# Windowed attention of a two-layer block: two heads' scores on the two halves of the array's rows, and transposed weights as the stationary operand against values laid high and low part side by side

## Chip, cores and metric

The kernel runs on one core of a Trainium2 chip, as one launch. The metric is the device time of that launch in microseconds (us). All arrays are float32. Products that must be exact to float32 are made from fp32r operands: a number is split into a high part (what a cast to fp32r keeps) and a low part (the rest), and three products, high·high, high·low and low·high, are summed in PSUM.

## The reference, cut to what matters

A block of depth 2 on 512 tokens and 256 context tokens, width 1024. Layer 0 has a gated MLP beside differential attention, layer 1 has the attention below; both are followed by a SwiGLU feed-forward stage (hidden 2816). Only layer 1's attention is touched:

```python
C_HEADS, C_KV_HEADS, HEAD_DIM, WINDOW, Q_BLOCK = 16, 4, 64, 128, 128   # 4 query heads to a key/value head
def sink_attend(q, kvs, sink):
    scores = []
    for k, v, mask in kvs:                      # the window's keys, then the 256 context keys
        s = einsum('bqhgd,bkhd->bhgqk', q, k) * ATTN_SCALE
        if mask is not None:
            s = where(mask, s, NEG_INF)
        scores.append(s)
    p = softmax(concatenate(scores + [s_sink], axis=-1), axis=-1)
    out = None                                  # sum over kvs of p's part @ v
    ...
def block(args):                                # one of 4 blocks of 128 queries
    kb, vb = 384 keys and values around the block      # 256 for the first and the last block
    mask = in range & (abs(qpos - kpos) <= WINDOW)
    return sink_attend(qb, [(kb, vb, mask), (kc, vc, None)], sink)
y = o.reshape(b, s_len, 1024) @ w_out
```

## The kernel before

Everything is kept transposed (features on partitions, tokens along the row). `odd()` is layer 1's mixer. It projects keys (`project_k`), values (six tiles of 128 tokens, one for each token block), and queries (`project_q(n)`, n = 0..7, two heads each: 24 products of 128x512 into the single PSUM bank of `fill()`). `attend(g, half)` then does one group of four heads (they share keys and values) for two of the four query blocks i. It calls `softmax(g, i, rc)` for the scores and the exponentials of the four heads x, and then goes over the key blocks kb, 4 of them for an edge block (i = 0 or 3) and 5 for an inner one (i = 1 or 2): 16 calls of `softmax`, 72 key blocks in all.

- Scores. `stack_q` puts one head's 64 high rows and 64 low rows on top of each other, `stack_k` writes the high keys on both halves and the low keys on both halves. A head's scores are then two products that use all 128 rows of the array, for the window's keys (L1150) and for the context's keys (L1158); window blocks other than the diagonal one get a mask added by a product of a mask with the identity (L1155). An edge block has 256 window keys, so one two-bank PSUM tile (`wide()`, two of them) holds two heads; an inner one has 384, and each head takes a `wide()` of its own. VectorE takes the row maximum (L1161), ScalarE the exponentials and their sums (L1164).
- Values. For each key block the four heads' exponentials are transposed into one PSUM bank (L1186, four products of 128x128), split into high part (ScalarE, L115) and low part (VectorE, L116), and multiplied by `mm3` (L99, L100, L101): the stationary operand is 64 columns of the values, the moving operand the 512 columns of four heads, and the output has 64 partitions.
- Normalization. The reciprocal sums are spread over 64 columns by GpSimd (L1197) and transposed (L1201); ScalarE copies the outputs out of PSUM (L1194) and VectorE multiplies (L1203). `keep` splits the result for the output projection `project(half, ...)`, products of 128x256 (L99 to L101 again, moving operand `ax`, weights through `blocks` and `unit`, whose splits are L75 and L78).

The order of instructions on each engine is set before the run by a list scheduler that works on the program with its own time estimates. It uses the output projection of half 0 and the query projections as filler between the attention's products. Tiles are handed out from pools; PSUM has 8 banks: three single ones (`bank()`, tiles `pb`), one `fill()` (`pf`), and two double ones (`wide()`, `pw`).

Of the kernel before, what the change touches and what calls it, by code (L numbers as in the profile page):

```python
# [6 lines left out]
F32 = mybir.dt.float32  # L7
# [7 lines left out]
P = 128  # L15
# [11 lines left out]
class Builder:  # L27
# [1042 lines left out]
    def odd(self):  # L1070
# [33 lines left out]
        vhi, vlo = [], []  # L1104
# [19 lines left out]
        def project_q(n):  # L1124
            ps = self.fill()
            self.dense(ps, self.blocks(a["q1"][n]), X)
            qf = Rs.tile([P, TX], F32, name=self.uid("qf"), tag="qf", bufs=2)
            self.rope(ps, qf, tabs)
            Qs[n] = self.stack_q(qf, Rs, TX, "sq", 16, 0.125)

        def softmax(g, i, rc):
# [9 lines left out]
            for x in range(4):  # L1141
                pair, par = x // 2, x % 2
                if edge:
                    two = self.wide() if par == 0 else two
                    ps = two[:, par * TX:par * TX + TX]
                else:
                    ps = self.wide()
                Q = Qs[2 * g + pair][par][:, i * P:(i + 1) * P]
                for p in range(2):
                    nc.tensor.matmul(ps[:, st:en], Q, K[g][p][:, b0 * P:b1 * P], start=p == 0, stop=p == 1,  # L1150
                                     skip_group_check=True)
                for b in range(b0, b1):
                    if b != i:
                        m0, c = (b - i + 1) * P, st + (b - b0) * P
                        nc.tensor.matmul(ps[:, c:c + P], identr, mask[:, m0:m0 + P], start=False, stop=True,  # L1155
                                         skip_group_check=True)
                for p in range(2):
                    nc.tensor.matmul(ps[:, en:en + TC], Q, K[g][p][:, TX:], start=p == 0 and not edge, stop=p == 1,  # L1158
                                     skip_group_check=True)
                c = nm[:, x:x + 1]  # L1160
                nc.vector.tensor_reduce(c, ps[:, st:en + TC], axis=AX, op=ALU.max, negate=True)  # L1161
                nc.vector.tensor_tensor(c, c, nsink[:, 4 * g + x:4 * g + x + 1], ALU.min)
                e = Rs.tile([P, 640], F32, name=self.uid("e"), tag="e1", bufs=7)
                nc.scalar.activation(e[:, :w + TC], ps[:, st:en + TC], AF.Exp, bias=c, accum_out=sums[:, x:x + 1])  # L1164
                es.append(e)
# [6 lines left out]
        def part(dtype=F32R):  # L1172
            return Rs.tile([P, 512], dtype, name=self.uid("pt"), tag="pt", bufs=6)

        def attend(g, half):
            raw[half, g] = Rs.tile([P, 2, TC], F32, name=self.uid("o"), tag="o", bufs=4)
            rc = self.small(8, "rc", 3)
            for i in (2 * half, 2 * half + 1):
                es, b0, b1 = softmax(g, i, rc[:, i % 2 * 4:i % 2 * 4 + 4])
                po = self.bank()[0:64, :]  # L1180
                nb = b1 - b0 + 2
                for kb in range(nb):
                    vb = b0 + kb if kb < b1 - b0 else 4 + kb - (b1 - b0)
                    pt = self.bank()
                    for x in range(4):
                        nc.tensor.transpose(pt[:, x * P:(x + 1) * P], es[2 * (x % 2) + x // 2][:, kb * P:(kb + 1) * P],  # L1186
                                            self.ident)
# [149 lines left out]
```

## Time and profile before

| what | value |
|---|---|
| median of the runs | 1698.41 us (1693.54 to 1702.56, 3 runs) |
| the profiled execution | 1697.54 us |
| its span, first to last instruction | 1695.8 us |
| TensorE busy, weight loads busy | 1558.7 us (92%), 1379.5 us (81%) |
| VectorE, ScalarE, GpSimd busy | 1145.4, 752.8, 806.8 us |
| mean granted TensorE clock | 0.972 |
| layer 1's attention in the span | about 1030 to 1250 us |

In the rows, PE is TensorE's products, PEld its weight loads (they overlap products), DVE VectorE, ACT ScalarE, POOL GpSimd. A product is shown as out<-moving operand, stationary operand (in alphabetical order), the rows and columns of the array that it uses (128*64), and the moving shape. The duration of one product contains its latency, so neighbours overlap; what a product costs TensorE is read from start to start in the timeline.

### The profile page before, as it was taken

Reading aid. Unit: us, or ns where it says so; the run is one execution under the profiler, and the core shown is the slowest. Engines: PE = TensorE matmul, PEld = TensorE weight load, DVE = VectorE, ACT = ScalarE, POOL = GpSimd, SP = SyncE. Lnnn points to the kernel's source line nnn. Section 1 sums busy time; section 2 is a strip of 40 time slices with the busy share of each in tenths; the row PEclk is TensorE's granted clock in tenths of the full one; section 3 lists DMA queues with packets and bytes.
Section 4 is the critical chain, followed back from the end, with each engine's and each line's share of the span. In section 5 each row is a group of like instructions: output and inputs, shape, how many; then the busy total and the mean of one; then the engine's idle time right before and its main releaser. Section 6 shows DMA issues by size and latency. Waiting matters only on the chain.

```text
span 1695.8 us, 24602 instructions
## 1 busy us (share of the span) xinstructions
PE 1558.7 (92%) x9415; PEld 1379.5 (81%) x9415; DVE 1145.4 (68%) x2037; ACT 752.8 (44%) x1521; POOL 806.8 (48%) x586
## 2 busy tenths in 40 slices
PE   6999989798899999999999988999987898999996
PEld 4776878698798889888899977778866788888986
DVE  4613788856967677666765676777769865756566
ACT  3413676433533233333333345676655444444443
POOL 0562211232675566656665336512115665666673
PEclk9999989899899899999999999999998999999998
DMA  8753100241032343344341112101140322222311
GB/s 312 290 184 133 32 1 1 87 159 41 25 125 88 124 136 110 127 136 135 132 132 38 49 63 75 51 7 45 50 146 10 125 90 98 87 100 78 110 38 50
DMA packets 47958, 161.98 MB, mean 96 GB/s; under 512 B 5472, under 2 KB 9952, under 8 KB 40160
## 3 DMA queue, kind: packets, MB, share of 16 engines
q1 hardware_dynamic: 47696, 160.28, 27.6%
q8 instruction: 74, 1.21, 0.3%
q14 instruction: 44, 0.36, 0.1%
q10 hardware_dynamic: 144, 0.13, 0.0%
HBM read 158.29 MB, written 2.10 MB: 95 GB/s over the span
## 4 chain that ended last, share of the span: by engine, by line
PE 65%; DVE 18%; DMA 6%; ACT 4%; issue 3%; POOL 3%; POOLq 0%; SPq 0%; DVEq 0%; ACTq 0%
PE pb L100 9%; PE pb L101 9%; PE pb L99 9%; PE pw L99 8%; PE pw L100 8%; PE pw L101 7%; DMA raw<-ffn_in 6%; POOL w L904 3%; DVE t L925 2%; PE pf L99 2%; PE pf L100 2%; PE pf L101 2%; PE pf L349 2%; DVE sq L925 1%; PE pb L1186 1%
## 5 line engine op out<-in xcount | busy, mean ns | idle before, releaser
L78 POOL TENSOR_TENSOR w<-raw,w 128x512 fp32r<-128x512 f32 (+1 forms) x84 | 128.6, 1540 | 234.3 <-ACT w L75 211.8
L99 PE MATMUL pw<-ax,w 128*128 128x384 f32 (+2 forms) x648 | 211.9, 331 | 18.0 <-DVE q L972 5.7
L904 POOL TENSOR_TENSOR w<-t,w 128x512 fp32r<-128x512 f32 x106 | 156.4, 1476 | 149.1 <-ACT w L901 146.0
L100 PE MATMUL pw<-ax,w 128*128 128x384 f32 (+2 forms) x648 | 210.7, 326 | 2.7 <-DVE ax L456 1.4
L101 PE MATMUL pw<-ax,w 128*128 128x384 f32 (+2 forms) x648 | 208.4, 324 | 3.1 <-DVE w L904 3.1
L757 DVE SCALAR_TENSOR_TENSOR xT<-pb,mod,xT 128x512 f32<-128x512 f32 (+3 forms) x208 | 143.9, 703 | 68.3 <-PE pb L101 67.9
L904 POOL TENSOR_TENSOR w<-raw,w 128x512 fp32r<-128x512 f32 x111 | 155.7, 1414 | 59.2 <-ACT w L901 59.2
L99 PE MATMUL pb<-hh,w 128*128 128x512 f32 x480 | 167.4, 363 | 14.8 <-ACT hh L115 7.9
L100 PE MATMUL pb<-hh,w 128*128 128x512 f32 x480 | 172.3, 361 | 0.7 <-POOL hh L116 0.2
L99 PE MATMUL pw<-T,w 128*128 128x384 f32 (+1 forms) x504 | 158.7, 318 | 12.2 <-DVE hs L968 9.5
L101 PE MATMUL pb<-hh,w 128*128 128x512 f32 x480 | 168.7, 359 | 0.0
L901 ACT CAST w<-t 128x512 fp32r<-128x512 f32 x120 | 74.2, 620 | 208.1 <-DVE t L925 176.8
L100 PE MATMUL pw<-T,w 128*128 128x384 f32 (+1 forms) x504 | 159.1, 316 | 7.0 <-DVE T L116 4.1
L101 PE MATMUL pw<-T,w 128*128 128x384 f32 (+1 forms) x504 | 158.3, 314 | 0.0
L99 PEld LDWEIGHTS pw<-ax,w 128*128 128x128 f32 x648 | 125.0, 194 | 32.8 <-DVE q L972 9.2
L100 PEld LDWEIGHTS pw<-ax,w 128*128 128x128 f32 x648 | 125.3, 193 | 10.5 <-DVE ax L193 3.3
L101 PEld LDWEIGHTS pw<-ax,w 128*128 128x128 f32 x648 | 124.8, 193 | 6.4 <-DVE w L904 3.3
L904 POOL TENSOR_TENSOR w<-rawo,w 128x512 fp32r<-128x512 f32 x74 | 107.2, 1448 | 39.1 <-ACT w L901 39.1
L99 PEld LDWEIGHTS pb<-hh,w 128*128 128x128 f32 x480 | 90.6, 191 | 28.5 <-ACT hh L115 9.0
L99 PEld LDWEIGHTS pw<-T,w 128*128 128x128 f32 x504 | 97.3, 194 | 18.9 <-DVE hs L968 11.9
L99 PE MATMUL pb<-ax,w 128*128 128x256 f32 (+1 forms) x344 | 106.8, 313 | 4.1 <-ACT w L75 2.2
L100 PE MATMUL pb<-ax,w 128*128 128x256 f32 (+1 forms) x344 | 106.3, 309 | 2.1 <-DVE ax L116 2.1
(381 smaller groups left out, 4324.4 us busy)
## 6 DMA issues: line engine op xcount, KB each, us to landing
raw<-ffn_in SPq DMA_DIRECT2D x44, 1024.0 KB, 5.7
ar<-ada SPq DMA_DIRECT2D x24, 1024.0 KB, 7.0
ar<-ada SPq DMA_DIRECT2D x48, 512.0 KB, 3.5
rawo<-ffn_out SPq DMA_DIRECT2D x44, 512.0 KB, 3.8
raw<-odd_out SPq DMA_DIRECT2D x32, 256.0 KB, 2.7
raw<-qk SPq DMA_DIRECT2D x16, 256.0 KB, 7.8
raw<-uv SPq DMA_DIRECT2D x16, 256.0 KB, 2.7
raw<-even_out SPq DMA_DIRECT2D x8, 512.0 KB, 3.5
```

What stands on the lines that cost most here:

```text
L78: eng.tensor_tensor(lo, raw, hi.bitcast(F32), ALU.subtract)
L99: mm(out, s[0], m[0], start=start, stop=False, **kw)
L100: mm(out, s[0], m[1], start=False, stop=False, **kw)
L101: mm(out, s[1], m[0], start=False, stop=stop, **kw)
L349: nc.tensor.matmul(ps[32 * q:32 * q + 32, :w], cst[:, k, :], t[:, w * q:w * q + w], start=k == 0, stop=k == KT - 1, skip_group_check=True)
L757: self.nc.vector.scalar_tensor_tensor(h, ps[:, r], self.modcol(l, j, m, who), h, ALU.mult, ALU.add)
L901: nc.scalar.copy(t[:, 0, :], src)
L904: eng.tensor_tensor(t[:, 1, :], src, t[:, 0, :].bitcast(F32), ALU.subtract)
L925: nc.vector.tensor_tensor(t, x, y, how)
L1186: nc.tensor.transpose(pt[:, x * P:(x + 1) * P], es[2 * (x % 2) + x // 2][:, kb * P:(kb + 1) * P], self.ident)
```

## The change

Three parts of `odd()` are rewritten. The reference's result is computed as before; only the product low·low, which the stacked scores included, is left out.

1. Queries are no longer stacked. High and low parts are two plain 128-row tiles, with one head of the pair on rows 0 to 63 and the other on rows 64 to 127 (one ScalarE and one VectorE instruction on 128 rows in place of two and two on 64). The scores of a pair of heads are made from three products of 64 rows each (high·high, high·low, low·high), for window and context keys: 12 products for the pair, which alternate between the two heads and so between the two halves of the array's rows; they were 8 of 128 rows. `issue_after` fixes their order among themselves. An inner block's pair needs both `wide()` tiles from its first two products on.
2. High and low values stand side by side (`v`, 64 + 64 columns for a group). For each head and key block, the transposed exponentials are now the stationary operand: the high part against 128 moving columns (both value parts), the low part against 64. A key block takes 8 products in place of 3.
3. The output now has queries on partitions. ScalarE copies the part that came from the low values, VectorE adds it to the other, GpSimd multiplies by the reciprocal sums, the result is transposed (as many transposes as the sums needed before) and ScalarE copies it out of PSUM.

```diff
         for tb in range(6):
-            hv, lv = [Rk.tile([P, TC], F32R, name=f"v1_{p}_{tb}") for p in range(2)]
-            self.split(hv, lv, acc[tb])
-            vhi.append(hv)
-            vlo.append(lv)
+            v = Rk.tile([P, 4, 2, 64], F32R, name=f"v1_{tb}")
+            self.split(v[:, :, 0, :], v[:, :, 1, :], acc[tb].rearrange("p (g d) -> p g d", d=64))
+            V.append(v)
...
-            Qs[n] = self.stack_q(qf, Rs, TX, "sq", 16, 0.125)
+            hi, lo = [Rs.tile([P, TX], F32R, name=self.uid("qs"), tag="sq", bufs=16) for _ in range(2)]
+            nc.scalar.mul(hi, qf, 0.125)
+            nc.vector.scalar_tensor_tensor(lo, qf, 0.125, hi.bitcast(F32), ALU.mult, ALU.subtract)
+            Qs[n] = hi, lo
...
-            for x in range(4):
-                pair, par = x // 2, x % 2
+            for pair in range(2):
                 if edge:
-                    two = self.wide() if par == 0 else two
-                    ps = two[:, par * TX:par * TX + TX]
+                    two = self.wide()
+                    pss = [two[:, h * TX:h * TX + TX] for h in range(2)]
                 else:
-                    ps = self.wide()
-                Q = Qs[2 * g + pair][par][:, i * P:(i + 1) * P]
-                for p in range(2):
-                    nc.tensor.matmul(ps[:, st:en], Q, K[g][p][:, b0 * P:b1 * P], start=p == 0, stop=p == 1,
-                                     skip_group_check=True)
...
-                for p in range(2):
-                    nc.tensor.matmul(ps[:, en:en + TC], Q, K[g][p][:, TX:], start=p == 0 and not edge, stop=p == 1,
-                                     skip_group_check=True)
...
+                    pss = [self.wide() for _ in range(2)]
+                last = None
+                for p, (qp, kp) in enumerate(((0, 0), (0, 1), (1, 0))):
+                    Q, Kp = Qs[2 * g + pair][qp], K[g][kp]
+                    for dst, src in ((slice(st, en), slice(b0 * P, b1 * P)), (slice(en, en + TC), slice(TX, TA))):
+                        for h, ps in enumerate(pss):
+                            r = slice(64 * h, 64 * h + 64)
+                            with tc.issue_after(last.ins) if last else ExitStack():
+                                last = nc.tensor.matmul(ps[:, dst], Q[r, i * P:(i + 1) * P], Kp[r, src],
+                                                        start=p == 0 and not (edge and dst.start == en), stop=p == 2,
+                                                        skip_group_check=True)
+                for h, ps in enumerate(pss):
+                    x = 2 * pair + h
...
-            rc = self.small(8, "rc", 3)
+            both = self.tmp("t")
             for i in (2 * half, 2 * half + 1):
-                es, b0, b1 = softmax(g, i, rc[:, i % 2 * 4:i % 2 * 4 + 4])
-                po = self.bank()[0:64, :]
+                rc = self.small(4, "rc", 3)
+                es, b0, b1 = softmax(g, i, rc)
+                po = self.bank().rearrange("p (x c d) -> p x c d", x=4, c=2)
...
                     self.split(th, tl, pt)
-                    V = [v[vb][:, 64 * g:64 * g + 64] for v in (vhi, vlo)]
-                    self.mm3(po, V, (th, tl), kb == 0, kb == nb - 1)
-                pov = po.rearrange("p (h a q) -> p h a q", h=2, q=P)
-                for par in range(2):
-                    nc.scalar.copy(raw[half, g][64 * par:64 * par + 64, :, i % 2 * P:i % 2 * P + P], pov[:, par, :, :])
+                    for x in range(4):
+                        c = slice(x * P, (x + 1) * P)
+                        nc.tensor.matmul(po[:, x, :, :], th[:, c], V[vb][:, g, :, :], start=kb == 0 and x == 0,
+                                         stop=False, skip_group_check=True)
+                        nc.tensor.matmul(po[:, x, 0, :], tl[:, c], V[vb][:, g, 0, :], start=False,
+                                         stop=kb == nb - 1, skip_group_check=True)
+                t = self.tmp()[:, :TC].rearrange("p (x d) -> p x d", d=64)
+                o = both[:, i % 2 * TC:i % 2 * TC + TC].rearrange("p (x d) -> p x d", d=64)
+                nc.scalar.copy(t, po[:, :, 1, :])
+                nc.vector.tensor_tensor(o, po[:, :, 0, :], t, ALU.add)
+                nc.gpsimd.tensor_tensor(o, o, rc.unsqueeze(2).to_broadcast([P, 4, 64]), ALU.mult)
             ps = self.bank()
-            rows = part(F32)
-            nc.gpsimd.tensor_copy(rows.rearrange("p (x d) -> p x d", d=64), rc.unsqueeze(2).to_broadcast([P, 8, 64]))
...
-            o = raw[half, g].rearrange("p a q -> p (a q)")
-            nc.vector.tensor_tensor(o, o, ps, ALU.mult)
+            raw[half, g] = Rs.tile([P, 2, TC], F32, name=self.uid("o"), tag="o", bufs=4)
+            nc.scalar.copy(raw[half, g].rearrange("p a q -> p (a q)"), ps)
```

In the changed kernel the score products are L1157, the masks L1165, the transposes L1194, the value products L1199 (high part) and L1201 (low part), the last transposes L1211.

The scheduler places the new products. On TensorE before, a key block in group 0 (`pt` are the split transposed exponentials, `v` the values, `e` the exponentials, `ident` the identity):

```order
L99 MATMUL pb_9406<-pt_9424,v_0_1_9241 64x512
L1186 MATMUL pb_9431<-ident_97,e_9372 128x128
L1186 MATMUL pb_9431<-ident_97,e_9391 128x128
L1186 MATMUL pb_9431<-ident_97,e_9381 128x128
L1186 MATMUL pb_9431<-ident_97,e_9400 128x128
L100 MATMUL pb_9406<-pt_9425,v_0_1_9241 64x512
L101 MATMUL pb_9406<-pt_9424,v_1_1_9242 64x512
```

On TensorE now, a key block of the same group, with the transposes of the next one behind it:

```order
L1199 MATMUL pb_9404<-v_4_9249,pt_9444 128x128
L1201 MATMUL pb_9404<-v_4_9249,pt_9445 128x64
L1199 MATMUL pb_9404<-v_4_9249,pt_9444 128x128
L1201 MATMUL pb_9404<-v_4_9249,pt_9445 128x64
L1199 MATMUL pb_9404<-v_4_9249,pt_9444 128x128
L1201 MATMUL pb_9404<-v_4_9249,pt_9445 128x64
L1199 MATMUL pb_9404<-v_4_9249,pt_9444 128x128
L1201 MATMUL pb_9404<-v_4_9249,pt_9445 128x64
L1194 MATMUL pb_9456<-ident_97,e_9370 128x128
L1194 MATMUL pb_9456<-ident_97,e_9375 128x128
L1194 MATMUL pb_9456<-ident_97,e_9393 128x128
L1194 MATMUL pb_9456<-ident_97,e_9398 128x128
```

Three products of 512 columns became eight of 128 and 64; the four transposes stay. The shapes shown are those of the output: 64 partitions before, 128 now.

On TensorE before, the scores of one head of an inner block (`kh` and `kl` are the stacked keys, `qb` the stacked queries):

```order
L1150 MATMUL pw_9493<-kh_8980,qb_9354 128x384
L1150 MATMUL pw_9493<-kl_8981,qb_9354 128x384
L1155 MATMUL pw_9493<-mask,identr 128x128 x2
L1158 MATMUL pw_9493<-kh_8980,qb_9354 128x256
L1158 MATMUL pw_9493<-kl_8981,qb_9354 128x256
```

On TensorE now, the scores of both heads of that pair, all but the first product (`qs_9345` is the high part, `qs_9346` the low part):

```order
L1157 MATMUL pw_9508<-kh_8980,qs_9345 128x384
L1157 MATMUL pw_9507<-kh_8980,qs_9345 128x256
L1157 MATMUL pw_9508<-kh_8980,qs_9345 128x256
L1157 MATMUL pw_9507<-kl_8981,qs_9345 128x384
L1157 MATMUL pw_9508<-kl_8981,qs_9345 128x384
L1157 MATMUL pw_9507<-kl_8981,qs_9345 128x256
L1157 MATMUL pw_9508<-kl_8981,qs_9345 128x256
L1157 MATMUL pw_9507<-kh_8980,qs_9346 128x384
L1157 MATMUL pw_9508<-kh_8980,qs_9346 128x384
L1157 MATMUL pw_9507<-kh_8980,qs_9346 128x256
L1157 MATMUL pw_9508<-kh_8980,qs_9346 128x256
L1165 MATMUL pw_9507<-mask,identr 128x128 x2
```

The two heads alternate (`pw_9507` is the one, on rows 0 to 63, `pw_9508` the other). The first product of the pair stands further ahead on TensorE, alone between products that use all 128 rows, where it waits for the first of the two `wide()` tiles only:

```order
L1199 MATMUL pb_9404<-v_1_9240,pt_9427 128x128
L1157 MATMUL pw_9507<-kh_8980,qs_9345 128x384
L99 MATMUL pf_10054<-ax_8611,w_10057 128x512
L100 MATMUL pf_10054<-ax_8612,w_10057 128x512
L101 MATMUL pf_10054<-ax_8611,w_10057 128x512
```

The 32 groups of 12 products stand in 55 uninterrupted stretches of the changed order; 32 of these come right behind transposes.

More of the change, by code (lines that the diff above doesn't have):

```diff
@@ L1185, in attend @@
                     for x in range(4):
[L1186 to L1187 removed]
+                        nc.tensor.transpose(pt[:, x * P:(x + 1) * P], es[x][:, kb * P:(kb + 1) * P], self.ident)
                     th, tl = [part() for _ in range(2)]
                     self.split(th, tl, pt)
[L1190 removed]
@@ L1198, in attend @@
             for i in range(2):
                 for pair in range(2):
-                    x = (i * 2 + pair) * P
-                    nc.tensor.transpose(ps[:, pair * TC + i * P:pair * TC + (i + 1) * P], rows[:, x:x + P], self.ident)
-            o = raw[half, g].rearrange("p a q -> p (a q)")
-            nc.vector.tensor_tensor(o, o, ps, ALU.mult)
+                    nc.tensor.transpose(ps[:, pair * TC + i * P:pair * TC + (i + 1) * P], both[:, i * TC + pair * P:i * TC + (pair + 1) * P],
+                                        self.ident)
```

29 lines of the change are left out of this document (14 added, 15 removed).

## The prediction

> **What bounds the kernel now.** First the page's busy times and the shares of the chain that ended last, to see which engine sets the end; then the stretches around layer 1's attention and TensorE's waits there.
>
> ```profile
> PE 1558.7 (92%) x9415; PEld 1379.5 (81%) x9415; DVE 1145.4 (68%) x2037; ACT 752.8 (44%) x1521; POOL 806.8 (48%) x586
> PE 65%; DVE 18%; DMA 6%; ACT 4%; issue 3%; POOL 3%; POOLq 0%; SPq 0%; DVEq 0%; ACTq 0%
> ```
>
> ```profile
> 1030.00:1070.00 40.00, 34.61 (x162) 28.65 (x163) 24.81 (x43) 17.71 (x36) 26.59 (x20) 0.96 0.22 66
> 1070.00:1210.00 140.00, 135.49 (x893) 112.88 (x892) 104.27 (x219) 95.62 (x224) 41.39 (x39) 1.00 0.13 39
> ```
>
> ```profile
> PE pf L99 <- DVE qf L244: 6.3, 5, 2.5
> PE pw L1150 <- ACT e L1164: 3.7, 9, 1.4
> ```
>
> The columns of the stretches are start and end, length, the busy time of PE, PEld, DVE, ACT and POOL (instructions in brackets), the granted clock and the DMA share. In the middle of the attention PE is busy 135.5 of 140 us at full clock, DVE 104, ACT 96. So TensorE is the bound there: time added to its products lengthens the kernel nearly one for one, and DVE and ACT have a quarter of the stretch to spare. The waits (total, times, longest, us, over 1030 to 1250) show what could be won otherwise: 10 us together, the larger part in the query projections, where the next projection needs the one `pf` bank that the rope still reads (L244).
>
> What a product costs TensorE is read from start to start:
>
> ```profile
> 1132.20 0.60 PE L1186 MATMUL pb<-ident,e 128*128 128x128 f32 x4
> 1132.55 0.36 PE L1150 MATMUL pw<-kh,qb 128*128 128x256 f32 x1
> 1132.76 0.28 PE L1150 MATMUL pw<-kl,qb 128*128 128x256 f32 x1
> 1132.87 0.22 PE L1155 MATMUL pw<-mask,identr 128*128 128x128 f32 x1
> 1132.93 0.33 PE L1158 MATMUL pw<-kh,qb 128*128 128x256 f32 x1
> 1133.10 0.28 PE L1158 MATMUL pw<-kl,qb 128*128 128x256 f32 x1
> 1133.22 0.40 PE L99 MATMUL pb<-pt,v 128*64 128x512 f32 x1
> 1133.45 0.39 PE L100 MATMUL pb<-pt,v 128*64 128x512 f32 x1
> 1133.68 0.39 PE L101 MATMUL pb<-pt,v 128*64 128x512 f32 x1
> 1133.91 0.27 PE L1186 MATMUL pb<-ident,e 128*128 128x128 f32 x1
> ...
> 1147.15 0.34 PE L1150 MATMUL pw<-kh,qa 128*128 128x384 f32 x1
> 1147.32 0.34 PE L1150 MATMUL pw<-kl,qa 128*128 128x384 f32 x1
> 1147.51 0.33 PE L1155 MATMUL pw<-mask,identr 128*128 128x128 f32 x2
> ```
>
> A 512-column product takes 0.23 us (1133.22 to 1133.91 is three), a 384-column one 0.18 (1147.15 to 1147.51 is two). The four from 1132.76 to 1133.22 take 0.115 each although one has 128 columns and three have 256: below 256 columns the moving operand no longer sets the price. A transpose takes 0.0875 (1132.20 to 1132.55 is four), and the product behind a run of transposes 0.21 in place of 0.115.
>
> **The values (part 2).** What sets 0.115 is seen in the weight loads (mean ns at the end of the first number group):
>
> ```profile
> L101 PEld LDWEIGHTS pf<-ax,w 128*128 128x128 f32 x120 | 23.1, 192 | 2.6
> L1186 PEld LDWEIGHTS pb<-ident,e 128*128 128x128 f32 x288 | 35.3, 140 | 10.7 <-DVE o L1203 0.4 <-ACT o L1194 0.4
> L101 PEld LDWEIGHTS pb<-pt,v 128*64 128x64 f32 x72 | 9.7, 135 | 1.9
> ```
>
> Loading 128 columns of an fp32r operand takes 192 ns, 64 columns of the values 135. Before, one short load fed 512 columns. Now the split exponentials are loaded, 128 columns each time, for 128 or 64 moving columns: every one of the eight products should cost the load-bound 0.115. A key block goes from 3 × 0.23 = 0.69 us to 8 × 0.115 = 0.92, and with 72 key blocks (the x72) that is 72 × 0.23 = **+16.6 us**. From below, the price is bounded by the transposes' 0.0875: 8 × 0.0875 = 0.70, +0.7 us in all. I take 0.115, since the mask is the nearest row: fp32r operands, 128 moving columns. No row has 64 moving columns; they need not cost more than the 128 of the mask.
>
> **The scores (part 1).** By the same prices, a pair of heads had 8 products: 8 × 0.115 = 0.92 us in an edge block, 4 × 0.18 + 4 × 0.115 = 1.18 in an inner one; there are 16 pairs of each. Now there are 12. If the two row halves work at the same time, they take the time of 6: 0.69 and 0.885, which saves 16 × 0.23 + 16 × 0.295 = **-8.4 us**. If they queue, 12 cost 1.38 and 1.77: +16.8 us. The masks stay as they are. No row of this trace has 64-row products, but layer 0's modulation puts four products side by side on column strips (128*32):
>
> ```profile
> 61.89 0.13 PEld L349 LDWEIGHTS pf<-ar,cst 128*32 128x32 f32 x4 [0.30 <-issue]
> 62.32 0.13 PEld L349 LDWEIGHTS pf<-ar,cst 128*32 128x32 f32 x4 [0.30 <-issue]
> ...
> 16.27 0.64 PE L349 MATMUL pf<-ar,cst 128*32 128x256 f32 x8
> 16.84 0.71 PE L374 MATMUL pw<-ar,ones 128*128 128x128 f32 x4
> 17.48 0.64 PE L349 MATMUL pf<-ar,cst 128*32 128x256 f32 x8
> ...
> 19.81 1.02 PE L175 MATMUL pb<-q,ones 128*128 128x512 f32 x2
> 20.76 0.64 PE L349 MATMUL pf<-ar,cst 128*32 128x256 f32 x8
> ```
>
> Groups of four with 512 columns follow each other every 0.43 us (61.89, 62.32), while one product of that kind on the whole array takes 0.475 (two from 19.81 to 20.76). So four strips cost the time of one, and their four loads fit into 0.13 us. I take the overlap for row halves too. [...]
>
> **Changing the array's division.** In the same rows a round of 8 strip products and 4 whole ones takes 1.21 us (16.27 to 17.48). The strips are two groups of 256 columns, half of 0.43 each, so 0.43; the four others 4 × 0.115 = 0.46; what is left, 0.32, is two changes, 0.16 each. The other bound is nothing: going to the values' 128*64 products and back costs no extra time (0.12 at 1133.10, 0.23 at 1133.68). The new scores stand in 55 stretches; each has an end, and 23 of them a beginning that is not behind transposes, where 0.1 is paid already. That is 78 changes, 0 to 12.5 us. With one near row on each side I take half, **+6.2 us**. [...]
>
> **Two PSUM tiles at once.** An inner pair now holds both `wide()` tiles.
>
> ```profile
> L1161 DVE TENSOR_REDUCE sa<-pw 128x1 f32<-128x640 f32 x32 | 26.0, 816 | 5.4 <-PE pw L1158 5.2
> L1164 ACT ACTIVATE e<-pw,sa 128x640 f32<-128x640 f32 x32 | 25.5, 796 | 8.0 <-DVE sa L1162 6.8 <-DVE sa L1168 0.5 <-PE pb L1186 0.3
> ```
>
> From the pair's last product to both tiles free: two maxima (1.63), the small step on the second and the exponentials (0.8), about 2.8 us. TensorE's own work beside one pair is half a block, 2.5 key blocks of 0.35 (transposes) + 0.92 = 3.2 us. That covers it on average by little, and the products queued behind a waiting L1157 (values, transposes, projections) wait along. Between nothing and 0.5 us for each of 16 pairs, 8 us, I take **+3**.
>
> **Queries and tail.** Splitting one projection's queries cost DVE two instructions on 64 rows; now it is one on 128, nearest row L193:
>
> ```profile
> L259 DVE SCALAR_TENSOR_TENSOR qa<-qf,qa 64x512 fp32r<-64x512 f32 x8 | 8.1, 1018 | 16.0 <-ACT qa L253 15.9
> L259 DVE SCALAR_TENSOR_TENSOR qb<-qf,qb 64x512 fp32r<-64x512 f32 x8 | 5.5, 687 | 0.2
> L193 DVE SCALAR_TENSOR_TENSOR ax<-t,mod,ax 128x512 fp32r<-128x512 f32 x8 | 5.9, 744 | 0.0
> ```
>
> That is 1018 + 687 - 744 = 0.96 us less ahead of the next rope, at five waits of L99 on L244: at most -4.8 us; half, **-2.4**, as not every wait stands behind it. At the end of the attention the last group goes through copy, add, multiplication, transposes and copy before `keep`:
>
> ```profile
> L1194 ACT COPY o<-pb 64x256 f32<-64x256 f32 x32 | 11.7, 365 | 9.1 <-PE pb L101 8.6
> L1203 DVE TENSOR_TENSOR o<-o,pb 128x512 f32<-128x512 f32 x8 | 5.4, 681 | 1.0 <-ACT o L1194 1.0
> L116 POOL TENSOR_TENSOR ax<-o,ax 128x256 fp32r<-128x256 f32 x11 | 8.0, 738 | 33.1 <-ACT ax L115 33.1
> ```
>
> Before: two copies and one multiplication, 1.4 us. Now, with 256-column steps of about 0.4 (ACT), 0.4 (DVE) and 0.74 (POOL), 0.2 for two transposes and 0.7 for a 512-column copy, 2.4: **+1** once, and nothing if the output projection's products, which need no result of the last group, hide it. In the earlier groups other groups' products hide it.
>
> **Sum.** 16.6 - 8.4 + 6.2 + 3 - 2.4 + 1 = +16.0 us on the profiled execution's 1697.5 (span 1695.8 plus 1.7 around it), 1713.5. The median is 0.9 us above that execution: **1714.4 us**.
>
> **Rivals.** A: the halves queue. For it: a 64-row load still has 128 columns, and this trace has no such row. The scores then cost +16.8 in place of -8.4: 1739.6. It decides as soon as a pair of an edge block takes over 0.92 us. B: the halves overlap, and neither the changes nor the PSUM tiles cost anything (as with 128*64 products): 16.6 - 8.4 - 2.4 + 1 = +6.8, 1705.2, no change. For it: the 10 us of waits, some of which longer products can fill. C, faster: weight loads of the split exponentials run at the transposes' pace, also 128 columns. The values cost +0.7, the scores -8.4, the queries up to -4.8, changes, tiles and tail nothing: -12.5, 1685.9. It decides where a key block's eight products stay under 0.69 us. Against it stands the 192 ns of every fp32r load. D: the new order itself waits more (values and maxima fall apart): beyond 1742.
>
> **How the numbers follow.** Forecast 0.50, A 0.19, B 0.17, C 0.11, D 0.03. A measurement of this kernel can tell about 0.5%, 8.5 us. The unknown prices alone carry the forecast from about +7 to +27 (changes 0 or 12.5, tiles 0 or 8). The range takes in B and A and leaves out C and D: 1700 to 1742. Slower by over 0.5% are the forecast, A and D; within 0.5% B; faster C.
>
> **What would show it.** Right: L1199 and L1201 starting every 0.115 us, a pair's L1157 starting in twos, a longer gap where L1157 begins or ends, PE busy for longer in the attention, and everything behind it shifted. Wrong: eight value products in 0.7 us (C), L1157 every 0.115 or more (A), or PE idle in front of L1157 for over 8 us (tiles).

## The result

| | before | after |
|---|---|---|
| median | 1698.37 us (1693.54 to 1702.56, 4 runs) | 1783.65 us (1773.07 to 1797.39, 4 runs) |
| profiled execution | 1697.54 us | 1797.39 us |
| span | 1695.8 us | 1794.9 us |
| mean granted TensorE clock | 0.972 | 0.926 |

The ratio is 1.0508 (1.0426 to 1.059): slower, 85 us against the 16 that were forecast, and outside the range. The profiled execution of after is the slowest of its four runs; the others have clocks of 0.931 to 0.936. Two kernels below (`e5_low128`, `e9_spread_low128`) spread by over 1.5% from run to run: their ratios leave out the runs furthest from their fastest, and their traces are of runs that are left out.

The page of after, busy times, granted clock in 40 slices (45 us each), and the chain:

```profile
PE 1655.3 (92%) x9903; PEld 1479.6 (82%) x9903; DVE 1134.6 (63%) x2037; ACT 746.0 (42%) x1505; POOL 810.9 (45%) x594
PEclk9999989899899999999999998657858899999998
PE 65%; DVE 16%; DMA 6%; POOL 5%; ACT 4%; issue 3%; POOLq 0%; SPq 0%; DVEq 0%; ACTq 0%
```

The same row of the page of before:

```profile
PEclk9999989899899899999999999999998999999998
```

Share of busy time and chain hardly differ from before: PE 92%, 65% of the chain. By these two lines nothing happened but more PE time. The clock row tells it: the six slices from 1077 to 1346 us stand at 8, 6, 5, 7, 8, 5 where before had 9, and they are the attention. The stretches of after (start and end, length, PE busy with products in brackets, granted clock, DMA share, GB/s):

```profile
1070.00:1100.00 30.00, 29.05 (x183) 1.00 0.18 54
1100.00:1140.00 40.00, 36.70 (x215) 0.68 0.04 14
1140.00:1180.00 40.00, 39.71 (x197) 0.54 0.03 7
1180.00:1220.00 40.00, 40.00 (x198) 0.50 0.00 0
1220.00:1260.00 40.00, 39.73 (x295) 0.87 0.15 47
```

From 1180 to 1220 PE is busy for 40.00 of 40 us, and the granted clock is 0.50: half speed, without a gap. The waits of PE between 1030 and 1350 (total, times, longest) are no larger than those of before (13 us in all, against 14 before from 1030 to 1250; three rows of them here):

```profile
PE pf L99 <- DVE qf L244: 5.6, 4, 2.5
PE pb L1201 <- DVE pt L116: 4.9, 8, 1.2
PE pw L1157 <- ACT e L1171: 0.9, 3, 0.4
```

The attention as a whole, from the first score product to the last transposes, before:

```profile
1039.30:1247.90 208.60, 196.24 (x1232) 1.00 0.15 49
```

and after:

```profile
1045.60:1350.40 304.80, 293.65 (x1739) 0.73 0.10 34
```

It grew by 96.2 us; the span by 99.1. (The first score product stands 6.3 us later, and what follows the attention is 3.4 us shorter.) Length times clock estimates the time that the same work would take at full clock; it scales the waits along, 13 us of the 304.80, so it is rough: 304.80 × 0.73 = 222.5 against 208.60, **+14 us**. The other 304.80 × 0.27 = **82 us is the clock**. These figures are of the profiled execution, 100 us slower than that of before; the medians are 85 us apart.

The single prices stand in the timeline of PE (start, duration, line). Where the clock is 1.00:

```profile
1078.74 0.30 PE L1199 MATMUL pb<-v,pt 128*128 128x128 f32 x1
1078.88 0.24 PE L1201 MATMUL pb<-v,pt 128*128 128x64 f32 x1
1078.96 0.30 PE L1199 MATMUL pb<-v,pt 128*128 128x128 f32 x1
...
1080.30 0.66 PE L1194 MATMUL pb<-ident,e 128*128 128x128 f32 x4
1080.88 0.44 PE L1157 MATMUL pw<-kh,qs 64*128 64x384 f32 x2
1081.11 0.33 PE L1157 MATMUL pw<-kl,qs 64*128 64x384 f32 x1
1081.16 0.28 PE L1157 MATMUL pw<-kh,qs 64*128 64x256 f32 x1
...
1081.95 0.66 PE L1165 MATMUL pw<-mask,identr 128*128 128x128 f32 x4
...
1136.92 0.45 PE L1199 MATMUL pb<-v,pt 128*128 128x128 f32 x1
1137.17 0.36 PE L1201 MATMUL pb<-v,pt 128*128 128x64 f32 x1
1137.35 0.45 PE L1199 MATMUL pb<-v,pt 128*128 128x128 f32 x1
```

A high and a low value product together take 0.22 us at 1078.74; the same pair takes 0.43 at 1136.92. Nothing waits in either place.

What changed in the surroundings is read from the groups by shape (count, busy time and mean ns) in one stretch, 1140 to 1180. Before:

```profile
L99 PE MATMUL pf<-ax,w 128*128 128x256 f32 x26 | 7.7, 295 | 0.0
L99 PE MATMUL pb<-pt,v 128*64 128x512 f32 x17 | 7.1, 418 | 0.0
```

After:

```profile
L1199 PE MATMUL pb<-v,pt 128*128 128x128 f32 x42 | 17.2, 430 | 0.0
L1201 PE MATMUL pb<-v,pt 128*128 128x64 f32 x43 | 15.0, 351 | 0.3 <-DVE pt L116 0.3
L99 PE MATMUL pf<-ax,w 128*128 128x256 f32 x2 | 1.0, 522 | 0.0
```

Before, 512-column value products and three lines of 256-column projections (26 on L99 alone) ran between the transposes. After, there are two on L99, and the rest is transposes, scores and products of 128 and 64 columns, each behind a load of 128 columns that takes 0.31 us (mean of the 84 loads of L1199 and L1201 there, at a mean clock of 0.54). So two things changed in that stretch: each product streams fewer columns for the time that it takes, and the projections that used to stand between them were used up earlier. Theories for the clock follow from that; the experiments tell them apart.

### The profile page after: what moved, and what is told of

Its sections match the earlier page's. It is cut to its first block, busy times and chain, and to the rows that moved or that the text cites. A ratio compares the mean times of both kernels' runs of the same rounds, so it can differ in the third digit from the quotient of the medians.

```text
span 1794.9 us, 25592 instructions
## 1 busy us (share of the span) xinstructions
PE 1655.3 (92%) x9903; PEld 1479.6 (82%) x9903; DVE 1134.6 (63%) x2037; ACT 746.0 (42%) x1505; POOL 810.9 (45%) x594
## 3 DMA queue, kind: packets, MB, share of 16 engines
q8 instruction: 77, 1.26, 0.3%
## 4 chain that ended last, share of the span: by engine, by line
PE 65%; DVE 16%; DMA 6%; POOL 5%; ACT 4%; issue 3%; POOLq 0%; SPq 0%; DVEq 0%; ACTq 0%
PE pb L100 7%; PE pb L99 7%; PE pb L101 7%; PE pw L99 7%; PE pw L100 7%; PE pw L101 7%; DMA raw<-ffn_in 6%; POOL w L904 3%; PE pb L1199 3%; PE pw L1157 3%; DVE t L925 2%; PE pf L99 2%; PE pb L1194 2%; PE pf L100 2%; PE pf L101 2%
## 5 line engine op out<-in xcount | busy, mean ns | idle before, releaser
L99 PE MATMUL pw<-ax,w 128*128 128x384 f32 (+2 forms) x648 | 212.4, 331 | 20.2 <-DVE q L972 8.1
L99 PE MATMUL pb<-hh,w 128*128 128x512 f32 x480 | 166.4, 361 | 13.6 <-ACT hh L115 8.0
L99 PE MATMUL pw<-T,w 128*128 128x384 f32 (+1 forms) x504 | 158.1, 317 | 9.9 <-DVE hs L968 6.5
L99 PEld LDWEIGHTS pw<-ax,w 128*128 128x128 f32 x648 | 125.1, 194 | 34.8 <-DVE q L972 11.6
L904 POOL TENSOR_TENSOR w<-rawo,w 128x512 fp32r<-128x512 f32 x74 | 105.8, 1429 | 38.5 <-ACT w L901 38.5
L99 PEld LDWEIGHTS pb<-hh,w 128*128 128x128 f32 x480 | 89.9, 190 | 27.1 <-ACT hh L115 9.1
L99 PE MATMUL pb<-ax,w 128*128 128x256 f32 (+1 forms) x344 | 109.0, 319 | 3.0 <-ACT w L75 1.6
L99 PEld LDWEIGHTS pw<-T,w 128*128 128x128 f32 x504 | 96.8, 193 | 16.5 <-DVE hs L968 8.5
L100 PE MATMUL pb<-ax,w 128*128 128x256 f32 (+1 forms) x344 | 107.9, 314 | 2.1 <-DVE ax L116 2.1
```

The costliest lines, as they stand in the source:

```text
L99: mm(out, s[0], m[0], start=start, stop=False, **kw)
L100: mm(out, s[0], m[1], start=False, stop=False, **kw)
L904: eng.tensor_tensor(t[:, 1, :], src, t[:, 0, :].bitcast(F32), ALU.subtract)
```

## The experiments

The theory, the author's: in this kernel the granted clock goes with how many moving columns go through the array per microsecond, and not with whether TensorE is busy (40.00 us of 40 at 0.50 above). The columns of one key block (four transposes of 128 columns, then the value products) by the time that it takes at full clock are the measure. Before, 4 × 128 + 3 × 512 = 2048 columns take 4 × 0.0875 + 3 × 0.23 = 1.04 us, 1970 per us. After, 512 + 4 × 192 = 1280 take 0.35 + 8 × 0.111 = 1.24, 1030 per us. The expectations also give this as a streamed share, of 2400 columns per us. That is an estimate, twice the pace at half clock: in the trace of before, seven products of 512 columns take 2.99 us from 1033.13 to 1036.12, at a granted clock of 0.50, so 1200 columns per us. The rivals: the 64-row score products or the changes of the array's division throttle it; the number of weight loads does; short waits do; or the order, without projections in between, does.

All kernels below are compared by the clock that they were granted from 1100 to 1220 us (columns as above). Before:

```profile
1100.00:1220.00 120.00, 115.95 (x794) 1.00 0.12 37
```

After:

```profile
1100.00:1220.00 120.00, 116.41 (x607) 0.58 0.02 7
```

### Each part alone

`e1_scores_only` is the kernel before with part 1 alone (queries, scores); `e2_values_only` is after with the queries and scores of before, thus parts 2 and 3 alone. The edit of `e2_values_only`, against after:

```diff
-            nc.scalar.mul(hi, qf, 0.125)
-            nc.vector.scalar_tensor_tensor(lo, qf, 0.125, hi.bitcast(F32), ALU.mult, ALU.subtract)
-            Qs[n] = hi, lo
+            Qs[n] = self.stack_q(qf, Rs, TX, "sq", 16, 0.125)
...
-                for p, (qp, kp) in enumerate(((0, 0), (0, 1), (1, 0))):
+                for p in range(2):
+                    nc.tensor.matmul(ps[:, st:en], Q, K[g][p][:, b0 * P:b1 * P], start=p == 0, stop=p == 1,
```

> Only part 1 of the change: 64-row score products, queries unstacked; values and normalization as before. Theory 1 (the clock follows how many columns are streamed through the array per time: the eight short value products stream 192 columns for every two weight loads, so the streamed share falls under about 0.4 and the clock to 0.50): the value products still stream 512 columns each, the clock in the attention stays at 1.00, and the time is 1690 to 1702 us (12 products took 1.08 us in an inner pair at full clock in the changed kernel against 1.18 before, 0.91 against 0.92 in an edge pair, queries up to -2.4). Theory 2 (the 64-row products and the changes of the array's division turn the clock down): granted clock 0.5 to 0.7 in the attention, 1740 us or more.

> Only parts 2 and 3: transposed weights stationary and the new normalization; scores stacked as before. Theory 1: the clock falls to 0.50 where no projection stands between, 1745 to 1790 us. Theory 2: the clock stays at 1.00 and only the longer value products are left, 1697 + 15 (72 key blocks of 0.89 in place of 0.69) = 1705 to 1718 us.

`e1_scores_only`: 1722.91 us, 1.0155 (1.0124 to 1.0186).

```profile
1100.00:1220.00 120.00, 109.40 (x740) 0.97 0.09 28
```

`e2_values_only`: 1722.26 us, 1.0145 (1.0111 to 1.018).

```profile
1100.00:1220.00 120.00, 113.30 (x940) 1.00 0.10 33
1110.00:1170.00 60.00, 54.26 (x439) 1.00 0.02 6
1250.00:1270.00 20.00, 18.96 (x108) 0.68 0.24 100
```

Each alone costs about 25 us, together they cost 85. Both times lie between the two that were expected, so neither theory's figure came. With either alone the clock stays near 1.00 in that stretch; in `e2_values_only` even from 1110 to 1170, where only 12 projection products stand, and it falls only at 1250 to 1270. So neither the 64-row scores nor the value products alone bring the clock down for good. The parts are not additive: only together do they bring the clock of that stretch to 0.58.

### More columns at the same loads

`e5_low128` is after with the low product run against both value parts, as the high one is: 128 moving columns in place of 64, so that low·low is added to the result. Loads, order and number of products stay.

```diff
-                        nc.tensor.matmul(po[:, x, 0, :], tl[:, c], V[vb][:, g, 0, :], start=False,
+                        nc.tensor.matmul(po[:, x, :, :], tl[:, c], V[vb][:, g, :, :], start=False,
```

> The whole change, but the low part of the weights is multiplied by both value parts (128 moving columns in place of 64; it adds the product low by low). The weight loads set the pace, so at full clock this costs nothing, and a key block streams 1536 columns with its transposes in place of 1280. Theory 1: the clock falls less, or not: 1715 to 1770 us. Theory 2: as the changed kernel, 1775 to 1790 us.

`e5_low128`: 1764.86 us (1739.15 at a mean clock of 0.968 to 1776.96 at 0.941), 1.0317 (1.0224 to 1.0409).

```profile
1100.00:1220.00 120.00, 112.35 (x840) 0.89 0.06 19
```

More work, less time: 512 + 4 × 256 = 1536 columns in the same 1.24 us, 1240 per us, and the clock in the row rises from 0.58 to 0.89.

### An added product, wide or narrow

`e3_fill512` adds one product per key block to after whose result is overwritten by the transposes; `e4_fill512x2` adds two. `e6_fill64` is the control, the same added product with 64 columns.

```diff
+                    for _ in range(1):     # e4_fill512x2: range(2); e6_fill64: 64 in place of 512
+                        nc.tensor.matmul(pt[:, :512], identr, K[g][0][:, :512], start=True, stop=True, skip_group_check=True)
```

> The whole change, and in each of the 72 key blocks one more product of 512 columns (identity by keys) into the bank that the transposes then overwrite; its result is used by nothing. This adds 72 x 0.23 = 16.6 us of work at full clock. Theory 1: 512 more columns in 1.25 us lift the streamed share from about 0.43 to 0.5 or more, the clock stays at or near 1.00, and the kernel gets faster in spite of more work: 1715 to 1745 us. Theory 2, or a clock that follows waits: no faster, 1780 to 1815 us.

> As the run with one added 512-column product in each key block, with two of them: 33 us of work more than the changed kernel at full clock, none of it used. Theory 1 (streamed columns per time set the clock): a key block with its transposes streams 2304 columns in about 1.7 us, share 0.56; the clock stays near 1.00 nearly throughout and the time is 1745 to 1765 us, under the changed kernel and not above the run with one. If more work only costs, 1785 us or more.

> Control for the two runs above: the added product has 64 columns in place of 512, with the same weight load, so nearly as many instructions and loads but few columns. Theory 1: the streamed share stays at 0.41 or less at full clock, the clock falls as in the changed kernel, and the time is 1780 to 1805 us. Theory 3 (the clock follows idle gaps or how densely instructions follow each other): as with the 512-column product or better, 1750 to 1770 us.

`e3_fill512`: 1768.77 us, 1.0428 (1.0384 to 1.0471).

```profile
1100.00:1220.00 120.00, 116.03 (x785) 0.83 0.05 14
```

`e4_fill512x2`: 1759.94 us, 1.0361 (1.0327 to 1.0394).

```profile
1100.00:1220.00 120.00, 116.35 (x894) 0.99 0.05 17
```

`e6_fill64`: 1790.9 us, 1.055 (1.0494 to 1.0606).

```profile
1100.00:1220.00 120.00, 115.00 (x634) 0.62 0.02 5
```

Adding 144 useless products of 512 columns, 0.23 us each or 33 us at full clock, makes after 24 us faster; 72 of them make it 15 us faster, less than was expected (1715 to 1745 us), and the slowest of these runs (1775.76) is not below the fastest of after (1773.07). The added product that has 64 columns hardly lifts the clock (0.62) and saves no time. It has the same place and the same load; what differs is its columns.

`e11_low128_fill512` puts `e5_low128` and `e3_fill512` together (both edits above).

> The whole change with both ways of streaming more columns: the low part of the weights against 128 columns (adds the product low by low, no more loads), and one unused 512-column product in each key block (72 x 0.23 = 16.6 us at full clock). A key block with its transposes then streams 2048 columns in 1.5 us, share 0.57. Theory 1: the clock stays at 1.00 nearly throughout and the time is 1725 to 1750 us: 1699 + 14 (the change at full clock) + 17 (added product), and little lost. That is faster than the same with one of the two alone (1769 and 1765 us). If the clock depends on something else: 1765 us or more.

1753.9 us, 1.0315 (1.0287 to 1.0344): 4 us above the expected interval, below `e3_fill512` and `e4_fill512x2`, but by its ratio not faster than `e5_low128` (1.0317).

```profile
1100.00:1220.00 120.00, 112.33 (x845) 0.94 0.05 16
```

### The old kernel, with other products

`e7_before_128` cuts each 512-column value product of before into four of 128: the same columns, four times as many loads.

```diff
-                    self.mm3(po, V, (th, tl), kb == 0, kb == nb - 1)
+                    for c in range(0, 512, P):
+                        s = slice(c, c + P)
+                        self.mm3(po[:, s], V, (th[:, s], tl[:, s]), kb == 0 and c == 0, kb == nb - 1)
```

> The kernel before, with each 512-column value product cut into four of 128 columns with the same stationary values: 12 loads and products for a key block in place of 3, the same columns streamed. Load-bound at 0.06 to 0.115 us each, a key block costs 0.72 to 1.38 us in place of 0.69, +2 to +50 us at full clock. Theory 1: the streamed share in the attention stays at about 0.5 or more, the clock at 1.00 in most of it, 1700 to 1755 us. Theory 4 (many weight loads, not few columns, turn the clock down): the clock falls to 0.50 and the time is above 1780 us.

1708.54 us, 1.0056 (1.0038 to 1.0074).

```profile
1100.00:1220.00 120.00, 113.72 (x1161) 1.00 0.12 36
```

A key block has 16 products and loads here, 12 in after; still the clock is 1.00. So the number of loads is not what brings it down here. From start to start the 864 products took 65.8 us, 0.076 each with the waits and the changes to other products, and 0.06 (median) from one to the next; both are below any price that the prediction had for a product.

`e12_before_diluted` adds 16 unused products of 16 columns, each with its own load of 128 columns, to each key block of before. The 512-column products, the projections and the 128-row scores stay.

```diff
+                    for _ in range(16):
+                        nc.tensor.matmul(pt[:, :16], identr, K[g][0][:, :16], start=True, stop=True, skip_group_check=True)
```

> The kernel before, with 16 unused products of 16 columns in each of the 72 key blocks, each with a full 128-column load of its own: few columns, much load time, 72 x 16 x 0.112 = 129 us of work at full clock. All other products keep their old shapes, on 128 rows. A key block with its transposes streams 2304 columns in 2.8 us, share 0.34. Theory 1: the clock falls to 0.50 in large parts of the attention, although the old products are all there, and the time is 1880 us or more. If only the new products' kinds (64 rows, weights as stationary operand) turned it down: clock 1.00, 1820 to 1840 us.

1867.14 us, 1.0963 (1.0915 to 1.101), between the two figures expected. Sixteen added products take 1.70 us from 1071.91 to 1073.61, at a clock of 1.00, so 0.11 each. 72 × 16 × 0.11 = 127 us would be their price at full clock; 169 was measured.

```profile
1100.00:1220.00 120.00, 119.52 (x724) 0.78 0.04 12
1380.00:1400.00 20.00, 20.00 (x98) 0.59 0.00 0
1400.00:1420.00 20.00, 18.77 (x77) 0.50 0.06 9
```

A kernel without a 64-row product and with before's value products falls to 0.50 too, and PE is busy for all of the 20 us from 1380 on while its clock is 0.59. So the slow clock belongs to no part of the change as such; here too it came with few columns for the time, 820 per us in a key block.

### The order alone

`e8_before_pair` gives before the order of the new scores and nothing else: the two heads of a pair alternate, and an inner pair holds both `wide()` tiles; the products are the 128-row ones of before.

```diff
-            for x in range(4):
-                pair, par = x // 2, x % 2
+            for pair in range(2):
...
+                    pss = [self.wide() for _ in range(2)]
```

> The kernel before, with the score products of a pair's two heads alternating as in the change, on all 128 rows and with stacked queries; an inner pair so holds both two-bank PSUM tiles at once. It tests where the 24 us of the run with the scores alone come from. If from the two tiles at once (longer waits of transposes and values for the exponentials): 1708 to 1722 us and waits of TensorE for ScalarE and VectorE some 8 us above before. If from the 64-row products and the changes of division: 1696 to 1703 us.

1709.94 us, 1.0066 (1.004 to 1.0092): +11 us. The stretch, and the waits from 1030 to 1280:

```profile
1100.00:1220.00 120.00, 108.79 (x746) 0.99 0.12 38
```

```profile
PE pb L1188 <- ACT e L1166: 8.7, 9, 1.7
PE pb L100 <- DVE pt L116: 6.7, 14, 1.1
```

PE is busy 7 us less in the stretch than before at the same clock: both heads' exponentials come late together, and transposes and values wait for them.

`e10_spread` is after with the query projections of a group held back behind the first value product of the group ahead, so that they stand among the value products. `e9_spread_low128` is the same with the edit of `e5_low128`.

```diff
+            with tc.issue_after(marks[n].ins) if n in marks else ExitStack():
+                self.dense(ps, W, X)
...
+                        if half == 0 and kb == 0 and x == 0:
+                            marks[2 * g + 2 + i] = first
```

> The whole change with the same instructions, only in another order: the 512-column products of the query projections of group g (g = 1 to 3) may not start before group g-1 has begun to multiply its values, so they stand between the attention's products in place of ahead of them. No work is added or removed. Theory 1 (streamed columns per time set the clock): in the first half of the attention the projections lift the streamed share to about 0.6 and the clock stays near 1.00 there, where the changed kernel ran at 0.50 to 0.86 from 1110 to 1230 us; the time falls to 1715 to 1755 us. If the clock follows anything in the products themselves (64-row products, their changes of division, the loads): no faster than the changed kernel, 1770 to 1800 us.

> The same order as the run before, and the low part of the weights against 128 columns in place of 64 (it adds the product low by low). Theory 1: the streamed share is higher in the second half of the attention too, the clock falls less there, and the time is 1710 to 1740 us, which is the full-clock cost of the change of about 14 us above before and some loss at the end. Not below before: the eight load-bound products stay.

`e10_spread`: 1797.47 us, 1.0572 (1.0527 to 1.0618). `e9_spread_low128`: 1789.3 us, 1.0507 (1.0433 to 1.058). Both times that the theory gave were missed by some 40 us or more, and `e10_spread` lies where it was expected if the clock follows the products themselves (1770 to 1800). The rows show why that does not decide it. Stretches and waits (1030 to 1350) of `e10_spread`:

```profile
1110.00:1125.00 15.00, 14.03 (x87) 1.00 0.17 54
1130.00:1145.00 15.00, 12.03 (x57) 0.61 0.00 0
1175.00:1225.00 50.00, 48.16 (x220) 0.50 0.01 4
```

```profile
PE pw L1167 <- ACT e L1173: 11.1, 7, 4.3
PE pb L1196 <- ACT e L1173: 7.7, 5, 1.6
```

The clock is 1.00 where projections stand and 0.50 to 0.61 between. Held back, they no longer cover the exponentials, and PE waits some 19 us for them; the half of the attention behind the projections is as it was. Moving the filler moves the places at full clock; it does not make more columns.

### The measure beside the clock

| kernel | columns per key block | us at full clock | columns per us | clock, 1100 to 1220 |
|---|---|---|---|---|
| before | 2048 | 1.04 | 1970 | 1.00 |
| e7_before_128 | 2048 | 1.26 | 1625 | 1.00 |
| e11_low128_fill512 | 2048 | 1.47 | 1390 | 0.94 |
| e4_fill512x2 | 2304 | 1.70 | 1355 | 0.99 |
| e5_low128 | 1536 | 1.24 | 1240 | 0.89 |
| e3_fill512 | 1792 | 1.47 | 1220 | 0.83 |
| after | 1280 | 1.24 | 1030 | 0.58 |
| e6_fill64 | 1344 | 1.35 | 1000 | 0.62 |
| e12_before_diluted | 2304 | 2.82 | 820 | 0.78 |

The times are worked out from 0.0875 for a transpose, 0.23 for 512 columns, 0.111 for a product behind a load of 128 columns (from start to start in after and, with 16 columns, in `e12_before_diluted`), and 0.076 in `e7_before_128`. Three rows stand out of order: `e11_low128_fill512` beside `e4_fill512x2` and `e6_fill64` beside after, by a little, and `e12_before_diluted`, whose projections still stand in the stretch. The table counts key blocks alone, and the columns of transposes once; scores and projections stand between them and are not in it: `e2_values_only` has after's key blocks, before's scores and a clock of 1.00.

## Why the prediction was wrong

**The step that failed** is the first reading: "PE is busy 135.5 of 140 us at full clock". The clock was read as a property of the stage, though it fell to 0.73 over the attention when other products ran in it, and all prices of the new products were taken at 1.00. The sum has no term for the clock, and none of the rivals A to D is about it. That left out 82 of the 96 us by which the attention grew. Rival D's "beyond 1742", at 0.03, is the only case that holds the time, but not by its mechanism: PE's waits did not grow, so the number was luck there.

**The sum at full clock came out near**: +16.0 forecast, +14 measured as length times clock. That is partly luck, as its terms were off in both directions (sums from start to start over the attention, from the kept traces):

- Values, 8 products at 0.115: the price is right, the gain against before is not. They start every 0.111 us (1078.74 to 1078.96 is two), and rival C fell with that. (The four starts that the 0.115 was read from are 0.11, 0.06, 0.17 and 0.12 apart, with the mask at 0.06, so that their mean fits is luck too.) But value products and transposes together, waits left out and at full clock, take 99.4 us in `e2_values_only` and 88.6 before: +10.8 in place of +16.6.
- Scores, -8.4, and changing the division, +6.2: the overlap is right, the gain is not. In the timeline above, the 11 products of an inner pair that stand together take 1.07 us with the change of the division behind them (1080.88 to 1081.95), and start in twos (1081.11 and 1081.16 are one of each head); one after the other, at 0.18 and 0.115, five of 384 and six of 256 columns would take 1.59. But added up, with 2 to 3 us of waits in each sum, score products and masks take 38.5 + 17.0 = 55.5 us in `e1_scores_only`, 45.2 + 7.3 = 52.5 before, and 39.3 + 12.2 = 51.5 in `e8_before_pair`, with 128-row products in the new order. That is +3 to +4 where -2.2 was forecast; the score products alone gain 6.7 us on before but 0.8 on `e8_before_pair`, and the masks behind them cost 4.8 us more than there. The transposes cost 5 us more than there as well (35.5 in `e1_scores_only` against 30.1 in `e8_before_pair`, waits left out): the last one ahead of a 64-row product lasts 0.21 us to its start (26 places), ahead of a 128-row one 0.04 (36 places). The prediction took the beginnings behind transposes as paid.
- Two PSUM tiles, +3: mis-sized. `e8_before_pair` measures the new order by itself at +11 us, above the upper end of 8. PE's waits in the attention are 21.6 us there, 12.4 before. The cover that the prediction counted, half a block of work by PE for each pair, may be there on average; at single pairs it is missing.
- Queries, -2.4: little of it came. The wait of L99 on L244 went from 6.3 to 5.6 us. The tail, +1, wasn't measured by itself.

In after part of these is not to be seen, as at half clock PE's own work covers the waits for ACT and DVE: its waits from 1030 to 1350 in the rows above come to 11 us, while `e8_before_pair` has 15 in two rows.

**How long the slow clock lasts.** At 0.50 the loads take longer too, 0.33 us (mean of L1199, 1180 to 1220) against 0.19 at 1.00 (1070 to 1100), and the pair of 0.43 us stands where one of 0.22 stood: 192 columns of the value products come to 450 per us in place of 870. From 1128 to 1231 the clock is lifted once, for 3.4 us, and it rises for 61 us (1230.67 to 1292.11) where the next projections stand:

```profile
1104.38:1107.79 3.41, 2.76 (x25) 1.00 0.29 77
1107.79:1121.44 13.65, 13.33 (x67) 0.50 0.01 2
1162.41:1165.81 3.40, 3.40 (x28) 1.00 0.26 77
1165.83:1230.67 64.84, 64.30 (x304) 0.50 0.00 1
```

The clock records of the two traces, 36 before and 46 after, hold only 0.50 and 1.00; what lies between in the rows are stretches that contain both. PE's busy time does not tell which of the two it is: the clock is 0.50 with PE busy for 40.00 of 40 us.

**Columns and clock, piece by piece.** The shortest time at one clock in these two traces is 3.413 us. Cut into pieces of that length, from 1030 to 1430 us, they give 236 pieces: 170 are followed by a piece at 1.00, and these hold 6230 columns in the median (2640 to 8450); 66 are followed by one at 0.50, and these hold 1890 (670 to 4860). All columns count once here, and a product's are spread over 0.23 us for 512, twice that at half clock. The two ranges overlap, so the count shows a tendency and no limit.

That after falls by its key blocks alone is not shown. Of its five falls between 1100 and 1340 four come behind pieces in which PE was busy for 1.84 to 2.76 of 3.41 us, as in the first row above; the one at 1165.81 comes behind 3.41 of 3.41. The rival of short waits is right that far: they stand ahead of most falls, but at 40.00 busy us of 40 there are none, and the clock stays at 0.50.

**What stays open.** What grants the clock, and at how many columns it changes: the runs show the tendency alone. `e1_scores_only` costs 13 us more than `e8_before_pair` (1722.91 against 1709.94). In the traces its attention is 14.5 us longer: 11 are PE's own work from start to start (the transposes 5 and scores with masks 3, as above), 3 its lower clock, and the waits are equal (21 us in each). What that work is beyond the changes of the array's division wasn't separated. No version that was run beats the kernel before.

## What to carry to other kernels

Here the granted clock went with the instruction mix of the stage (1.00 before and 0.58 after, 1100 to 1220 us), so a change that turns wide moving operands into many narrow ones must be priced with the clock as an unknown: count the moving columns per us of full-clock time, before and after, over a few microseconds, and ask what stands between. Ask how long a slow clock lasts, too: in after it stood at 0.50 from 1165.83 to 1230.67, with PE busy for 64.30 of 64.84 us. Swapping the stationary and the moving operand does the same arithmetic, but here 768 columns in 0.89 us replaced 1536 in 0.69. When a kernel slows down while the busy shares and the waits stay, look at the clock row first, and multiply length by clock to see which part of the loss is work.

## What the runs showed of the hardware

- TensorE at half clock while busy without a gap: 0.50 over 40.00 busy us of 40 (after, 1180 to 1220).
- Work that isn't needed can save time: 144 added products of 512 columns made after 24 us faster (1759.94 against 1783.65), 72 of 64 columns did not (1790.9).
- A product of 128 moving columns with a 64-column load starts every 0.06 to 0.076 us (`e7_before_128`), against 0.111 for 128 and 64 columns with a 128-column load (after, 1078.74 to 1078.96), and 0.11 for 16 (`e12_before_diluted`): here the price goes with the load.
- Pieces of 3.413 us that were followed by a clock of 1.00 held 6230 columns in the median, those followed by 0.50 held 1890 (236 pieces of before and after, the ranges overlap).
- Products on the two halves of the rows ran at the same time: 11 in 1.07 us, change of the division included (after, 1080.88 to 1081.95), where 1.59 was the price one after the other.
